# An order edge between each product of keys and receptances and the next, so that the halves of TensorE's rows take turns

## The chip, the cores and the metric

The kernel runs on one core of one Trainium2 chip. The metric is device time in microseconds (us). Times of the kernel before come from three runs; the profile is one more execution, and every duration below is from it.

## The reference

The model has seven stages over 256 tokens of width 2048, one batch, all float32: an RWKV-7 mixer (layer 0), a dilated attention (1), a pooling mixer (2), a second RWKV-7 mixer (3), a layer of attention and a linear recurrence (4), an mLSTM layer (5) and a final norm (6). The change lies in the two RWKV-7 mixers, in the part that computes this scan for 32 heads of 64:

```python
def _rwkv7_scan(r, w, k, v, a, b):
    """All inputs (B,S,H,N) float32. State S (B,H,N_v,N_k):
    S_t = S_{t-1} diag(w_t) + (S_{t-1} a_t) b_t^T + v_t k_t^T ;  y_t = S_t r_t."""
    ...
    def step(state, inp):
        r_t, w_t, k_t, v_t, a_t, b_t = inp
        sa = jnp.einsum('bhij,bhj->bhi', state, a_t)
        state = (state * w_t[:, :, None, :] + sa[..., None] * b_t[:, :, None, :]
                 + v_t[..., None] * k_t[:, :, None, :])
        y_t = jnp.einsum('bhij,bhj->bhi', state, r_t)
        return state, y_t
```

Around it stand four input projections (2048 x 2048 each, for r, k, v and the gate g), small low-rank products for decay and gates, a norm per head and an output projection (2048 x 2048).

## The kernel before

**Projections.** `proj` (L262) multiplies in three fp32r products (high by high, high by low, low by high). Each weight block of 512 KB is fetched by a DMA queued on SyncE (`wr`), split by ScalarE into its high part (`wh`, L220) and by VectorE, in the RWKV layers at times GpSimd, into its low part (`wl`, L221), and feeds 12 products of 128x128 by 128x512 on TensorE. These products are the filler of TensorE's queue through the whole program.

**The scan by blocks.** `rwkv_block` treats 4 heads (256 columns) at a time, so a layer has 8 blocks; `rwkv_blocks` starts one about every 40 us of the planner's time, and several are under way at once. The 256 tokens of a block are 4 chunks of 64. A block computes its decays and gates; builds `AR` (receptances and removal keys, scaled) and `BK` (keys and their counterparts, scaled), last of all by GpSimd (L811); computes the bonus product into the PSUM tile `qb` (L824), which ScalarE copies out as `bon` (L828); multiplies `BK` by `AR` within each chunk (L838, the lines of the change); masks the result into `GM` on VectorE (L841); copies the small diagonal blocks to `Md` (ScalarE, L856); inverts them by a recurrence on VectorE (L867 to L877), a product chain (L925, L952) on TensorE; and walks over the chunks (L986 to L1018). `yt` is then normed and joined into `z` (L1032 to L1053), transposed (L277) and used by `w_out`, the output projection. Block 7's part of `z` feeds only the last quarter of `w_out`.

**The products of L838.** The two heads of a pair lie on partitions 0 to 63 and 64 to 127. For each pair `f` (0, 1) there are 8 products, chunk c = 0..3 by half hp = 0, 1; each contracts over 64 rows, so it uses one half of TensorE's rows. The four of a half go to one PSUM tile (`qs[hp]`), and `qs` are of the pool `tp`, which has two banks. `tp` also holds `qb`, the transposes (L277, L785) and the low-rank products (L720). A float32 product is two passes on the chip, so the profile counts 512 passes for the 2 layers x 8 blocks x 2 pairs x 8 products = 256.

**What sets the order.** The program text is not the order of the queues. A scheduler (the tile framework, with a timeline model) places each instruction on its engine's queue when its inputs are ready by its model, by priority; blocks of the scan have a high priority (`urgent`). Queues then run in order on the chip.

Of the kernel before, what the change touches and what calls it, by code (L numbers as in the profile page):

```python
# [23 lines left out]
ORDER = mybir.DependencyInfo(mybir.DependencyClass.NoSync, mybir.DependencyReason.DATA)  # L24
# [90 lines left out]
class Builder:  # L115
# [558 lines left out]
    def rwkv_block(self, ia, b):  # L674

        nc, I, S = self.nc, self.I, self.S
# [89 lines left out]
        AR = self.t("q4", [128, 2, 4, 128], F32, 8)  # L766
        BK = self.t("q4", [128, 2, 4, 128], F32, 8)
# [54 lines left out]
        for t in range(2):  # L822
            for f in range(2):
                nc.tensor.matmul(qb[:, t * 4 + f * 2:t * 4 + f * 2 + 2], pr[:, f, t * 128:t * 128 + 128], rkc[:, f],  # L824
                                 start=True, stop=True)
# [6 lines left out]
        gmask = self.c("gmask")  # L832
        for f in range(2):
            qs = [self.p("tp", (128, 4, 128)) for _ in range(2)]
            for c in range(4):
                for hp in range(2):
                    rs = slice(hp * 64, hp * 64 + 64)
                    nc.tensor.matmul(qs[hp][:, c], BK[rs, f, c], AR[rs, f, c], start=True, stop=True)  # L838
            self.pe(0.9)
            for hp in range(2):  # L840
                nc.vector.tensor_tensor(GM[:, f * 2 + hp].rearrange("p (q a) n -> p q (a n)", a=2),  # L841
                                        qs[hp].rearrange("p (q a) n -> p q (a n)", a=2),
                                        gmask[:, f * 128:f * 128 + 256].unsqueeze(1).to_broadcast([128, 2, 256]), OP.mult)
            yield 1.0
# [7 lines left out]
        for i in range(4):  # L852
            rs = slice(i * 32, i * 32 + 32)
# [115 lines left out]
        rows = self.bcast(I["a_rows"][ia, b, 256:768], "rows", 512, 1)  # L969
# [3 lines left out]
        for c in range(4):  # L973
# [18 lines left out]
            for hp in range(2):  # L992
                for f in range(2):
                    nc.tensor.matmul(gy[ar[f], 4 + hp], X[ar[f], (f * 2 + hp) * 2 + pq], G[ar[f], f, hp],
                                     start=first, stop=True, skip_group_check=True)
# [5 lines left out]
            if c < 3:  # L1001
                for hh in range(4):
                    f, hp = hh // 2, hh % 2
                    nc.tensor.matmul(gy[half[hp], 6 + f], BT[:, f * 3 + c, half[hp]], UV[:, hh * 64:hh * 64 + 64],
                                     start=first, stop=True, skip_group_check=True)
# [10 lines left out]
            for hh in range(4):  # L1016
                f, hp = hh // 2, hh % 2
                nc.tensor.matmul(gy[kr[f], hh], GM[:, hh, c, to[f]:to[f] + 64], UV[:, hh * 64:hh * 64 + 64],  # L1018
                                 start=first, stop=True, skip_group_check=True)
# [838 lines left out]
```

## Time and profile before

| | us |
|---|---|
| median of three runs | 3241.56 |
| the three runs | 3240.18, 3241.56, 3243.27 |
| profiled execution, its own time | 3250.24 |
| its span, first to last instruction | 3247.1 |
| TensorE busy | 3034.3 (93%) |
| VectorE busy | 2304.0 (71%) |
| ScalarE busy | 1783.2 (55%) |
| mean granted TensorE clock | 0.967 |

The profiled execution took 8.7 us more than the median, and 3.1 us of it lie outside the span. Layer 0's scan runs from about 180 to 740 us of the span, layer 3's from about 1800 to 2400 us. Views of the profile name an instruction by its line, its engine, and the tiles that it writes and reads, buffer numbers left out. PE is TensorE, PEld its weight loads, DVE VectorE, ACT ScalarE, POOL GpSimd. An engine's busy time counts a product until its modelled end, so the step from one start to the next start is the better measure of what a run of products occupies.

### The profile page before, as it was taken

The page shows a single profiled execution, that of the slowest core. Times are in us where ns is not written, and L with a number is a line of the kernel's source. Part 1 is how long each engine was busy: PE and PEld are TensorE (multiplying, and loading weights), DVE is VectorE, ACT ScalarE, POOL GpSimd, SP SyncE. Part 2 cuts the span into 40 slices and gives each one's busy share as a digit, 9 for nine tenths or more (in the row PEclk, how much of TensorE's full clock was granted, in tenths as well). Part 3 has the DMA queues.
Part 4 walks back from the last instruction along what each step waited for, and adds up shares of the span by engine and source line. Part 5 has one row for each costly group of instructions (what it writes and reads, how often), then busy time and mean ns, then how long its engine had stood idle before and what let it go on. Part 6 is the DMA issues. An engine that isn't in the chain of part 4 may idle for free. (4 is left out here: it accounts for less than half of the span.)

```text
span 3247.1 us, 48857 instructions
## 1 busy us (share of the span) xinstructions
PE 3034.3 (93%) x17128; PEld 2452.2 (76%) x17128; DVE 2304.0 (71%) x4623; ACT 1783.2 (55%) x3504; POOL 794.6 (24%) x614
## 2 busy tenths in 40 slices
PE   6889999998999999999978898998989999999998
PEld 4667677776888888888856776777777788888886
DVE  7778778765666666676597788788557775666765
ACT  4565555444555555655555565554456765555554
POOL 4433443440112111020054325434312110000101
PEclk9999999999999999999989998999999999999999
DMA  5654453366666656666656644533665566666665
GB/s 186 200 193 145 155 175 121 122 200 203 178 174 178 177 169 205 205 211 191 208 174 219 197 152 153 171 119 105 206 214 160 156 188 203 182 199 172 186 187 169
DMA packets 327014, 577.24 MB, mean 178 GB/s; under 512 B 33856, under 2 KB 60776, under 8 KB 326768
## 3 DMA queue, kind: packets, MB, share of 16 engines
q1 hardware_dynamic: 326768, 574.12, 57.4%
q8 instruction: 134, 2.20, 0.3%
q14 instruction: 112, 0.92, 0.1%
HBM read 527.88 MB, written 46.15 MB: 177 GB/s over the span
## 5 line engine op out<-in xcount | busy, mean ns | idle before, releaser
L221 DVE TENSOR_TENSOR wl<-wr,wh 128x512 fp32r<-128x512 f32 x1580 | 1179.0, 758 | 690.8 <-ACT wh L220 664.3
L220 ACT CAST wh<-wr 128x512 fp32r<-128x512 f32 x1728 | 1052.4, 620 | 976.2 <-PE qps L262 452.9
L262 PE MATMUL qps<-wl,ah 128*128 128x512 f32 x3424 | 1385.8, 405 | 39.1 <-DVE wl L221 38.2
L262 PE MATMUL qps<-wh,al 128*128 128x512 f32 x3424 | 1368.7, 400 | 1.3 <-DVE al L221 1.3
L262 PE MATMUL qps<-wh,ah 128*128 128x512 f32 x3424 | 1266.3, 405 | 45.7 <-ACT wh L220 13.2
L262 PEld LDWEIGHTS qps<-wh,ah 128*128 128x128 f32 x3424 | 656.5, 192 | 191.0 <-ACT st L596 15.4
L262 PEld LDWEIGHTS qps<-wl,ah 128*128 128x128 f32 x3424 | 659.0, 192 | 187.2 <-DVE wl L221 53.3
L262 PEld LDWEIGHTS qps<-wh,al 128*128 128x128 f32 x3424 | 657.5, 192 | 137.9 <-DVE al L221 2.7
L221 POOL TENSOR_TENSOR wl<-wr,wh 128x512 fp32r<-128x512 f32 x148 | 203.6, 1385 | 363.9 <-ACT wh L220 336.3
L1103 POOL TENSOR_TENSOR q<-q,gain 128x1024 f32<-128x1024 f32 (+1 forms) x15 | 35.0, 2332 | 376.5 <-ACT sq L1097 376.5
L321 POOL TENSOR_TENSOR rstd<-rs_v,mhalf 128x2 f32<-128x2 f32 x7 | 5.0, 708 | 430.6 <-DVE rs_v L319 430.5
L277 PE MATMUL qtp<-cst,q 128*128 128x128 f32 x388 | 62.0, 289 | 23.0 <-DVE al L295 6.8
L838 PE MATMUL qtp<-q,q 64*128 64x128 f32 x512 | 72.4, 306 | 7.5 <-DVE GM L841 3.8
L277 PEld LDWEIGHTS qtp<-cst,q 128*128 128x128 f32 x388 | 48.5, 148 | 36.5 <-issue 20.5
L485 DVE SCALAR_TENSOR_TENSOR e<-q,vec,q 128x256 f32<-128x256 f32 x96 | 73.7, 811 | 0.0
L872 DVE TENSOR_TENSOR mb<-mb,Xc 128x120 f32<-128x120 f32 (+14 forms) x240 | 73.1, 305 | 0.1
L838 PEld LDWEIGHTS qtp<-q,q 64*128 64x128 f32 x512 | 57.9, 201 | 18.3 <-POOL q L811 5.1
L221 DVE TENSOR_TENSOR al<-st,ah 128x512 fp32r<-128x512 f32 x64 | 54.7, 871 | 23.5 <-ACT ah L220 23.4
L856 ACT COPY Md<-GM 32x128 f32<-32x128 f32 x128 | 55.3, 432 | 27.7 <-DVE GM L841 26.4
L220 ACT CAST ah<-st 128x512 fp32r<-128x512 f32 x64 | 38.3, 617 | 57.6 <-DMA st<-mix 49.7
L875 DVE TENSOR_TENSOR Xc<-Xc,mb 128x8 f32<-128x8 f32 x240 | 59.2, 247 | 1.1
L487 POOL TENSOR_TENSOR e<-e,q 128x512 f32<-128x512 f32 x32 | 48.2, 1521 | 31.8 <-ACT e L483 27.0
(388 smaller groups left out, 3383.2 us busy)
## 6 DMA issues: line engine op xcount, KB each, us to landing
wr<-a_w_in SPq DMA_DIRECT2D x256, 512.0 KB
wr<-b_w_in SPq DMA_DIRECT2D x160, 512.0 KB
wr<-odd_w_in SPq DMA_DIRECT2D x128, 512.0 KB
wr<-even_w_in SPq DMA_DIRECT2D x72, 512.0 KB
wr<-a_w_out SPq DMA_DIRECT2D x64, 512.0 KB
wr<-c_w_in SPq DMA_DIRECT2D x64, 512.0 KB
st<-mix SPq DMA_DIRECT2D x64, 256.0 KB
wr<-c_w_out SPq DMA_DIRECT2D x32, 512.0 KB
```

What stands on the lines that cost most here:

```text
L220: self.nc.scalar.copy(hi, src)
L221: (eng or self.nc.vector).tensor_tensor(lo, src, hi.bitcast(F32), OP.subtract)
L262: nc.tensor.matmul(o[:, cs], u[:, kk, sl], v[k][:, cs], start=st and x == 0 and c1 == 0, stop=sp and x == 2, skip_group_check=True)
L277: nc.tensor.transpose(q[:, f, t * 128:t * 128 + 128], src[:, t, (fp * 2 + f) * 128:(fp * 2 + f) * 128 + 128], self.ident)
L321: nc.gpsimd.tensor_tensor(r, v, self.mhalf[:, 0:2], OP.pow)
L485: ins = nc.vector.scalar_tensor_tensor(m[:, f], st.xx[c][:, ft], mu, st.h[c][:, ft], OP.mult, OP.add)
L487: ins = nc.gpsimd.tensor_tensor(m, m, st.h[c][:, a * 2:a * 2 + 2], OP.add)
L838: nc.tensor.matmul(qs[hp][:, c], BK[rs, f, c], AR[rs, f, c], start=True, stop=True)
L856: nc.scalar.copy(Md[rs, :, us].rearrange("p c u -> p u c"), GM2[rs, us, (1 - i // 2) ^ f, rs])
L872: nc.vector.tensor_tensor(mb[:, 0:n], mb[:, 0:n], Xc[:, r:r + 1].to_broadcast([128, n, 8]), OP.mult)
L875: nc.vector.tensor_tensor(Xc[:, r + 1], Xc[:, r + 1], mb[:, 0], OP.add)
L1103: nc.gpsimd.tensor_tensor(e3, e3, gain.unsqueeze(1).to_broadcast([128, 2 * nh, 128]), OP.mult)
```

## The change

Each product of L838 gets an order edge to the one before it within its pair `f`. The edge is between instructions of one engine, with no semaphore; it only tells the scheduler that the second may not be placed ahead of the first. As the loop goes over hp within c, the halves of the rows take turns: 0, 1, 0, 1, and so on. In the changed kernel the products are at L839, and all lines behind them stand 4 higher.

```diff
         for f in range(2):
             qs = [self.p("tp", (128, 4, 128)) for _ in range(2)]
+            turn = None
             for c in range(4):
                 for hp in range(2):
                     rs = slice(hp * 64, hp * 64 + 64)
-                    nc.tensor.matmul(qs[hp][:, c], BK[rs, f, c], AR[rs, f, c], start=True, stop=True)
+                    mm = nc.tensor.matmul(qs[hp][:, c], BK[rs, f, c], AR[rs, f, c], start=True, stop=True)
+                    if turn is not None:
+                        self.tc.add_manual_dep(mm.ins, turn.ins.name, ORDER, reason="the halves of the rows take turns")
+                    turn = mm
             self.pe(0.9)
```

No instruction is added or removed, on any engine. The scheduler's result moves between the first block and the end of the scan in each of the two layers, on all five queues; outside these two stretches the queues are the same but for a handful of rows. In TensorE's queue of 14,374 products, the 256 products of L838 stand in 71 unbroken runs before and in 64 now. Within the runs, 119 products followed one of the same half before, and none does now.

The first place is TensorE's queue at block 2 of layer 0, first pair: `qtp_3355` and `qtp_3356` are its two halves. Before, first the one half,

```order
L1004 MATMUL qgy_2362<-uv_2366,q4_2155 64x64 x4
L262 MATMUL qps_2058<-wh_2268,ah_1827 128x512
L262 MATMUL qps_2058<-wl_2269,ah_1827 128x512
L262 MATMUL qps_2058<-wh_2268,al_1828 128x512
L262 MATMUL qps_2057<-wh_2339,ah_1920 128x512
L838 MATMUL qtp_3355<-q4_3221,q4_3222 128x128 x4
```

and 22 products later the other, the four of a half together each time:

```order
L262 MATMUL qps_2058<-wl_2344,ah_1920 128x512
L262 MATMUL qps_2058<-wh_2343,al_1921 128x512
L262 MATMUL qps_2057<-wh_2398,ah_1920 128x512
L262 MATMUL qps_2057<-wl_2399,ah_1920 128x512
L262 MATMUL qps_2057<-wh_2398,al_1921 128x512
L262 MATMUL qps_2058<-wh_2398,ah_1920 128x512
L262 MATMUL qps_2058<-wl_2399,ah_1920 128x512
L838 MATMUL qtp_3356<-q4_3221,q4_3222 128x128 x4
L925 MATMUL qgm_2932<-Y_2930,GM_2689 64x64 x5
```

Now the first product stands at about the same place, alone, and the other seven follow 155 products later, behind work of the blocks before (L956 is the old L952, L998 the old L994):

```order
L998 MATMUL qgy_2501<-G_2507,X_2209 64x64 x4
L956 MATMUL qgm_3041<-X_2928,W_3005 32x32 x15
L839 MATMUL qtp_3356<-q4_3221,q4_3222 128x128
L839 MATMUL qtp_3355<-q4_3221,q4_3222 128x128
L839 MATMUL qtp_3356<-q4_3221,q4_3222 128x128
L839 MATMUL qtp_3355<-q4_3221,q4_3222 128x128
L839 MATMUL qtp_3356<-q4_3221,q4_3222 128x128
L839 MATMUL qtp_3355<-q4_3221,q4_3222 128x128
L839 MATMUL qtp_3356<-q4_3221,q4_3222 128x128
```

What moved is the completion of the first pair. Before, both halves went one after the other through one bank of `tp` while the other bank still held `qb`; now both banks are needed at once, and the second product waits for `bon`'s copy out of `qb`. In 12 of the 16 blocks 20 or more products stand between the first product of the first pair and its second (20 to 155).

The second place is ScalarE's queue at the copy `bon` of block 1 of layer 0. Before:

```order
L903 COPY AV_2161<-qgm_2162 128x512
L828 COPY bon_2687<-qtp_2682 128x8
L220 CAST ah_1827<-st_1829 128x512
L220 CAST ah_1827<-st_1833 128x512
L220 CAST wh_1906<-wr_1904 128x512
L911 COPY q4_2155<-qgm_2185 128x384
L220 CAST wh_1910<-wr_1904 128x512
L856 COPY Md_2738<-GM_2689 32x4x32 x4
```

Now (L907, L915 and L860 are the old L903, L911 and L856):

```order
L907 COPY AV_2161<-qgm_2162 128x512
L915 COPY q4_2155<-qgm_2180 128x384
L828 COPY bon_2687<-qtp_2682 128x8
L220 CAST ah_1827<-st_1833 128x512
L220 CAST wh_1906<-wr_1904 128x512
L220 CAST wh_1910<-wr_1904 128x512
L220 CAST wh_1961<-wr_1959 128x512
L915 COPY q4_2155<-qgm_2185 128x384
L220 CAST wh_1965<-wr_1959 128x512
L860 COPY Md_2738<-GM_2689 32x4x32 x4
```

The copies `Md` moved back against `bon`. Before, the first `Md` copy stood ahead of `bon` in 6 of the 16 blocks (2, 3, 6 and 7 of layer 0, 2 and 4 of layer 3); now `bon` is first in all of them.

The third place is the end of each scan in TensorE's queue, told in counts. Layer 0: between block 7's last chunk product (L1018) and the transposes of its `z` (L277) stood 72 products of L262, and now 98; the chunk product itself stands at the same place as before. Layer 3: there stood 91, and now 59; the chunk product stands 72 products later than before.

## Rows read from the trace of the kernel before

**Rows 1.** The page: the span, and busy time of each engine over it.

```profile
span 3247.1 us, 48857 instructions
PE 3034.3 (93%) x17128; PEld 2452.2 (76%) x17128; DVE 2304.0 (71%) x4623; ACT 1783.2 (55%) x3504; POOL 794.6 (24%) x614
```

**Rows 2.** Stretches of both scans: length, busy us by engine, PEclk granted clock, DMA.

```profile
core 0: us, PE busy (x) PEld busy (x) DVE busy (x) ACT busy (x) POOL busy (x), PEclk, DMA share, GB/s
...
180.00:740.00 560.00, 519.66 (x3989) 408.25 (x3988) 435.16 (x1201) 297.83 (x653) 228.09 (x184) 0.95 0.50 157
...
1800.00:2400.00 600.00, 549.02 (x4134) 432.18 (x4133) 455.55 (x1260) 316.27 (x690) 236.54 (x187) 0.94 0.52 165
```

**Rows 3.** ScalarE's waits, 1800 to 2400: who for whom, us, times, longest.

```profile
ACT wh L220 <- PE qps L262: 82.2, 67, 6.1
```

**Rows 4.** The page's groups of L838: busy, mean ns of one, idle before, releaser.

```profile
L838 PE MATMUL qtp<-q,q 64*128 64x128 f32 x512 | 72.4, 306 | 7.5 <-DVE GM L841 3.8 <-POOL q L811 3.7
...
L838 PEld LDWEIGHTS qtp<-q,q 64*128 64x128 f32 x512 | 57.9, 201 | 18.3 <-POOL q L811 5.1 <-issue 4.9 <-DVE GM L841 4.2
```

**Rows 5.** Timeline of PE, 183.7 to 185.8: start, us, instruction, count.

```profile
183.71 0.39 PE L262 MATMUL qps<-wh,al 128*128 128x512 f32 x1
183.94 0.39 PE L262 MATMUL qps<-wh,ah 128*128 128x512 f32 x1
184.25 1.16 PE L838 MATMUL qtp<-q,q 64*128 64x128 f32 x16
185.34 0.50 PE L262 MATMUL qps<-wl,ah 128*128 128x512 f32 x1
185.69 0.39 PE L262 MATMUL qps<-wh,al 128*128 128x512 f32 x1
```

**Rows 6.** Timeline of PE at two runs of a single half.

```profile
1962.04 0.49 PE L838 MATMUL qtp<-q,q 64*128 64x128 f32 x2 [0.16 <-POOL q L811]
1962.46 0.71 PE L986 MATMUL qgy<-S,q 128*128 128x128 f32 x4
...
2229.72 1.16 PE L838 MATMUL qtp<-q,q 64*128 64x128 f32 x8
2230.80 0.50 PE L262 MATMUL qps<-wh,ah 128*128 128x512 f32 x1
```

**Rows 7.** Timeline of block 2 in layer 0: bonus product, L838, mask, `bon`.

```profile
260.29 0.95 PE L824 MATMUL qtp<-rkc,e 128*128 128x2 f32 x8
...
269.11 1.16 PE L838 MATMUL qtp<-q,q 64*128 64x128 f32 x8 [0.88 <-POOL q L811]
277.10 0.68 DVE L841 TENSOR_TENSOR GM<-qtp,cst 128x512 f32<-128x512 f32 x1
...
277.83 1.16 PE L838 MATMUL qtp<-q,q 64*128 64x128 f32 x8 [2.15 <-DVE GM L841]
...
292.41 0.17 ACT L828 COPY bon<-qtp 128x8 f32<-128x8 f32 x1
```

**Rows 8.** Stretches behind two such waits, columns as in Rows 2.

```profile
225.00:233.00 8.00, 6.17 (x39) 4.80 (x41) 7.37 (x11) 5.71 (x14) 6.19 (x6) 0.57 0.55 172
277.00:284.00 7.00, 5.84 (x55) 4.70 (x56) 5.50 (x11) 3.47 (x8) 0.00 (x0) 0.76 0.36 117
```

**Rows 9.** Timeline at the ends of both scans: last chunk product, `z`, its transposes.

```profile
713.44 0.46 PE L1018 MATMUL qgy<-uv,GM 128*64 128x64 f32 x8
...
733.39 0.65 PE L277 MATMUL qtp<-cst,z 128*128 128x128 f32 x4 [2.43 <-DVE z L1051]
734.68 0.77 PE L262 MATMUL qps<-wh,ah 128*128 128x512 f32 x1 [0.64 <-ACT ah L220]
...
2339.52 0.46 PE L1018 MATMUL qgy<-uv,GM 128*64 128x64 f32 x8
...
2361.03 0.68 DVE L1051 SCALAR_TENSOR_TENSOR z<-yt,z 128x512 f32<-128x512 f32 x1
2363.88 0.60 PE L277 MATMUL qtp<-cst,z 128*128 128x128 f32 x4
```

## The prediction

> **What bounds the kernel now.** I read the page first, then the stretches, then the waits. The page gives TensorE 93% of the span [rows 1], so time taken from it is the first candidate for time gained. The change touches only two stretches, the scans of layers 0 and 3. There TensorE is busy 519.7 of 560 us and 549.0 of 600 us, 92 to 93%, and VectorE 435.2 and 455.6 us, 76 to 78% [rows 2]. The weight splits tell which of the two leads: in layer 3's stretch ScalarE waited 82.2 us for TensorE to let go of weight buffers [rows 3], its largest wait there. The feed is ahead of TensorE more often than behind it. So a microsecond less of TensorE's work is mostly a microsecond less of time, but not wholly: the 7 to 8% in which TensorE stood idle are waits on VectorE, ScalarE and DMAs, which stay as long as they are.
>
> L838 itself is busy 72.4 us over both layers, with 7.5 us of idle time before it [rows 4].
>
> **What taking turns saves.** Eight products (16 passes) whose halves alternate occupy TensorE from 184.25 to 185.34, 1.09 us [rows 5]. Four products (8 passes) of one half occupy it from 2229.72 to 2230.80, 1.08 us, and one product alone from 1962.04 to 1962.46, 0.42 us [rows 6]. So a further product of the same half costs (1.08 - 0.42) / 3 = 0.22 us, a run has 0.20 us of its own, and two products of different halves next to each other cost what one costs: eight in turns are four steps, 0.20 + 4 x 0.22 = 1.08, as measured. Around a run the neighbours lose a little: L262 products start 0.23 apart, but 0.31 passes before the run and 0.35 after it [rows 5], so 0.08 + 0.12 = 0.20 us more. A run costs 0.40 us plus 0.22 for each step.
>
> Counting the runs of the two orders with each alternating pair as one step, I find 217 steps in 71 runs before and 149 steps in 64 runs now. That is 68 x 0.22 = 15.0 us, and 7 x 0.40 = 2.8 us, together 17.8 us less of TensorE's work. It isn't the 256 to 128 steps that the idea suggests: four of the 32 groups alternated fully before, others in part, and now the first product of a group often stands alone, which makes a run and a step of its own.
>
> [...]
>
> How much of the 17.8 us becomes time? The ends are nothing (another engine or a chain's latency takes each microsecond) and all of it. With TensorE busy for 92% of both stretches and the weight splits waiting for it [rows 2, 3], I take three quarters: **13.4 us less**.
>
> **What the new order costs inside the scans.** Before, the two halves of a group could use one bank of `tp` after the other: in block 2 the second half waited 2.15 us for the mask of the first [rows 7]. This wait, 3.8 us in all [rows 4], goes, since both halves finish together. In its place the second product waits for the copy `bon`. In block 2 of the kernel before, that copy came at 292.41, 32 us after its product at 260.29, and it delayed nothing then [rows 7]; now the whole group hangs on it. TensorE's queue runs in order, so if `bon` is late, the products of all blocks under way and L262 stand behind it, and then VectorE's masks and the `Md` copies. The scheduler has put the second product far back for this (12 blocks with 20 to 155 products in between), so by its model the wait is over. [...] Below nothing, the old mask waits bring 3.8. [...] I take **2 us more**: one or two late copies, less the mask waits. The value is near the low end, since ScalarE is busy about half of these stretches (297.8 of 560 us, 316.3 of 600 [rows 2]) and `bon` is a copy of 0.17 us [rows 7].
>
> **The ends of the scans.** From the last chunk product to the finished `z` it took 19.9 us in layer 0 (713.44 to the wait's end near 733.3) and 22.2 us in layer 3 (2339.52 to 2361.03 + 0.68) [rows 9]. This chain is on VectorE, ScalarE and GpSimd and does not get shorter. TensorE covers it with L262. In layer 0 the cover was 72 products, which ended 2.43 us too early, and a wait of 0.64 us came behind [rows 9]. Now it is 98 products, at least 98 x 0.23 = 22.5 us, so the 3 us of waiting go: **3 us less**, and the slower clock behind them is left as a reserve. In layer 3 the cover was 91 products in 24.4 us, 0.27 each, and hid the chain. Now it is 59: 13.6 us at 0.23 each, 15.9 at 0.27. TensorE then waits between 19.9 - 15.9 = 4.0 and 22.2 - 13.6 = 8.6 us, with up to 1.7 us of slow clock behind it as after the other waits [rows 8]. I take **6 us more**, near the middle.
>
> **Edits at nothing.** The edges add no semaphore and no instruction. The rows of the DMA queue that changed places fetch the same weights; the shared cover for them is the three buffers of `wr`. Should this fail, it shows as ScalarE waiting for `wr`.
>
> **The sum.** -13.4 + 2 - 3 + 6 = -8.4 us. Against the profiled execution's own 3250.2 us (the span is 3247.1) this gives 3241.8; the median lay 8.7 us below that execution, so on its side I expect 3241.6 - 8.4 = 3233.2, say 3233 us. About 0.2%, 6.5 us, is what a measurement of this kernel can tell from no change, so the forecast lies just beyond it.
>
> **Rivals.**
>
> *The gain is taken by the feed (no change).* VectorE is at 76 to 78% in the scans and has the recurrence and all the low parts of the weights in one queue [rows 2]. If TensorE's saved time only lengthens its waits on them, the conversion is a quarter: -4.5 + 2 - 3 + 6 = +0.5 us, 3242 us. For it: the rescheduled queues differ everywhere in the scans, and 7 to 8% of idle time shows that a block's latency already counts. Against it: the 82 us that the splits waited for TensorE [rows 3].
>
> [...]
>
> *The edges don't do what they say.* The order of the changed kernel excludes it: all 32 groups read 0, 1, 0, 1.
>
> *The gain is whole.* With all 17.8 us, no late copy and the mask waits gone: -17.8 - 3.8 - 3 + 4 = -20.6, 3221 us. It is the low end of the forecast rather than a case of its own.
>
> **How the numbers follow.** Forecast, a gain of 7 to 21 us: 0.46. No change: 0.28. Slower by the late copies or a longer uncovered end in layer 3: 0.26. The range reaches from the whole gain, with 3 us for what the clock gives back, 3218, to a little below the slower rival's time, 3256, so that about one in ten lies on either side. The forecast's own range is 3218 to 3235, and the other two cases hold more than half of the chance together. Chances: faster by over 0.2% 0.46, within 0.2% 0.28, slower by over 0.2% 0.26.
>
> **What would show it.** In the profile after, L839's busy time should fall from 72.4 us to about 50 to 56, and whole groups of 16 passes should take 1.1 us. TensorE's wait for the mask (`GM`) should be gone. [...] Before the `z` transposes of layer 3's block 7 a wait of 4 to 9 us should stand, and in layer 0 none. TensorE's other idle time in the two stretches should not grow by more than about 4 us; if it grows by 13, the feed has taken the gain. The prediction would be wrong from the ground if L839's time didn't fall, or if the two stretches took the same time with less work in them.

## The result and the profile after

The changed kernel took **3277.41 us** (median of four runs, 3273.34 to 3279.61) against 3242.41 for the kernel before in the same batch: ratio 1.0105, 95% interval 1.0088 to 1.0122. It is 35 us slower, where 8 us faster was forecast. Repeated in a later batch it took 3272.26, ratio 1.0084 [1.0057, 1.0111].

The page after, span and busy time, to hold against [rows 1]:

```profile
span 3274.1 us, 48894 instructions
PE 3021.2 (92%) x17128; PEld 2434.5 (74%) x17128; DVE 2320.2 (71%) x4623; ACT 1784.4 (55%) x3504; POOL 797.1 (24%) x614
```

TensorE works 13.1 us less and the span is 27.0 us longer, so its idle time grew by 40.1 us (212.8 to 252.9). (The two profiled executions differ by 27 us and the medians by 35, since the one of the kernel before lay 8 us above its median.) VectorE works 16.2 us more, with the same instructions. The page's groups say where (line, engine, tiles, shapes, count, busy us, mean ns, idle before and releaser). After:

```profile
L876 DVE TENSOR_TENSOR mb<-mb,Xc 128x120 f32<-128x120 f32 (+14 forms) x240 | 80.4, 335 | 0.2
L879 DVE TENSOR_TENSOR Xc<-Xc,mb 128x8 f32<-128x8 f32 x240 | 77.4, 323 | 0.9
...
L839 PE MATMUL qtp<-q,q 64*128 64x128 f32 x512 | 52.7, 299 | 5.4 <-POOL q L811 3.2
```

and the same two VectorE groups in the kernel before:

```profile
L872 DVE TENSOR_TENSOR mb<-mb,Xc 128x120 f32<-128x120 f32 (+14 forms) x240 | 73.1, 305 | 0.1
L875 DVE TENSOR_TENSOR Xc<-Xc,mb 128x8 f32<-128x8 f32 x240 | 59.2, 247 | 1.1
```

The products fell from 72.4 [rows 4] to 52.7 us, as the change meant them to. The recurrence on VectorE rose from 132.3 to 157.8 us, 25.5 more, though it does the same.

Most of the loss lies in layer 3. The operation `sq` of ScalarE starts for the first time in layer 1, behind layer 0's scan, and for the last time in layer 4, behind layer 3's. Its line gives both starts, before and then after:

```profile
L1097 ACT ACTIVATE sq<-q x15: 656/1067/1098, 816.7 to 2567.7; 128x1024 f32<-128x1024 f32 x14, 128x512 f32<-128x512 f32 x1
```

```profile
L1101 ACT ACTIVATE sq<-q x15: 656/1067/1097, 822.9 to 2594.7; 128x1024 f32<-128x1024 f32 x14, 128x512 f32<-128x512 f32 x1
```

The program is 6 us late behind the first scan and 27 us behind the second.

The view of TensorE's waits says what the new idle time waits for (who for whom: us, times, longest). Kernel before, 180 to 745:

```profile
PE qgm L925 <- DVE Y L934: 2.6, 2, 1.5
PE qtp L277 <- DVE z L1051: 2.4, 1, 2.4
PE qgy L994 <- DVE G L989: 2.3, 3, 1.2
```

After, the same stretch (L998, L929 and L990 are the old L994, L925 and L986):

```profile
PE qgy L998 <- DVE X L959: 11.3, 2, 6.8
PE qgm L929 <- DVE Y L938: 10.3, 4, 8.8
PE qgy L998 <- DVE G L993: 6.7, 3, 3.9
...
PE qps L262 <- DVE st L387: 5.2, 1, 5.2
PE qgy L990 <- DVE S L1019: 5.1, 2, 3.5
```

All five are waits for VectorE, four of them in the inverse and the chunk walk of a block. The wait for `X` did not exist before. Other rows fell: before, the chunk walk's wait for `uv` (L1004) was the largest with 7.2 us, and now it is 0.8; all rows of the stretch together grew from 39.7 to 61.4 us. In layer 3 (1800 to 2440) they grew from 54.6 to 70.1, and the largest row there, before and then after, is a wait for a DMA, of weights for the low-rank products:

```profile
PE qtp L720 <- DMA lw<-a_a2x: 12.8, 7, 3.4
```

```profile
PE qtp L720 <- DMA lw<-a_a2x: 20.0, 7, 6.0
...
PE qtp L839 <- ACT bon L828: 2.1, 1, 2.1
```

The second row is the wait for `bon`, which the forecast feared: TensorE stood for it once in the whole program, 2.1 us. Yet `bon` is where the delay begins. Timeline of block 2 of layer 0, first pair, to hold against [rows 7]:

```profile
272.83 0.49 PE L839 MATMUL qtp<-q,q 64*128 64x128 f32 x2
...
291.98 1.04 POOL L1033 TENSOR_TENSOR vt<-vt,bon 128x512 f32<-128x512 f32 x1 [6.39 <-ACT uv L984]
...
293.06 0.17 ACT L828 COPY bon<-qtp 128x8 f32<-128x8 f32 x1 [0.44 <-POOL vt L1033]
...
298.31 1.16 PE L839 MATMUL qtp<-q,q 64*128 64x128 f32 x14
...
299.30 1.29 DVE L845 TENSOR_TENSOR GM<-qtp,cst 128x512 f32<-128x512 f32 x2
```

`bon` has two buffers, so the copy of block 2 needs the buffer that block 0 still uses: it starts 0.04 us after GpSimd's last use of it (L1033, `vt` times `bon`, at the end of block 0's chunk walk). The pair is complete at 299.5; before, it was complete at 279.0. TensorE is not idle meanwhile, since the scheduler put other work there; the block is late instead. In 7 of the 12 blocks that have a block two ahead, `bon` now starts within 0.4 us after that block's last use; before, in 3.

Before, in blocks 2, 3, 6 and 7 of layer 0, both pairs were done when `bon` came, since the halves passed through the bank that `qb` did not hold. In block 2 the second pair ended at 289.2, and `bon` came at 292.41 [rows 7]:

```profile
288.68 0.49 PE L838 MATMUL qtp<-q,q 64*128 64x128 f32 x2
```

The recurrence began only 2.1 to 5.3 us after `bon` in these four blocks. Now first pair, masks, `Md` copies and second pair all stand behind the copy, and it begins 17.1 to 24.9 us after `bon` in all 16 blocks. So the blocks follow each other more slowly: from the recurrence of block 0 to that of block 7 it took 408.2 us in layer 0 and 407.8 in layer 3, and now 418.7 and 438.2.

That moves a block's recurrence to the time when GpSimd norms the output of the block two ahead (`yt`, L1038 to L1049). A piece of block 3's recurrence beside block 1's `yt`, timeline of VectorE and GpSimd after:

```profile
384.84 1.28 POOL L1047 TENSOR_TENSOR yt<-yt,rows 128x512 f32<-128x512 f32 x1
...
385.00 1.15 DVE L879 TENSOR_TENSOR Xc<-Xc,mb 128x8 f32<-128x8 f32 x1
...
386.20 0.20 DVE L876 TENSOR_TENSOR mb<-mb,Xc 128x56 f32<-128x56 f32 x1
386.20 1.35 POOL L1048 TENSOR_TENSOR yt<-yt,rows 128x512 f32<-128x512 f32 x1
...
386.44 1.13 DVE L879 TENSOR_TENSOR Xc<-Xc,mb 128x8 f32<-128x8 f32 x1
...
387.62 0.20 DVE L876 TENSOR_TENSOR mb<-mb,Xc 128x48 f32<-128x48 f32 x1
...
387.85 0.17 DVE L879 TENSOR_TENSOR Xc<-Xc,mb 128x8 f32<-128x8 f32 x1
```

The `Xc` operation by itself took 0.17 us here, and the two beside a GpSimd operation took 1.13 and 1.15; each ended just behind that one (386.15 behind 386.12, 387.57 behind 387.55). Of the 480 operations of these two groups 73 took over 0.6 us, 47 before, and every one of them overlaps a GpSimd operation. Of these, 26 lie longest beside `yt`, 7 before; the others lie mostly beside the low parts `wl` (40, and 34 before).

### The profile page after: what moved, and what is told of

It reads as the page before. It is cut to its first block, busy times and chain, and to the rows that moved or that the text cites. A ratio compares the mean times of both kernels' runs of the same rounds, so it can differ in the third digit from the quotient of the medians.

```text
span 3274.1 us, 48894 instructions
## 1 busy us (share of the span) xinstructions
PE 3021.2 (92%) x17128; PEld 2434.5 (74%) x17128; DVE 2320.2 (71%) x4623; ACT 1784.4 (55%) x3504; POOL 797.1 (24%) x614
## 5 line engine op out<-in xcount | busy, mean ns | idle before, releaser
L262 PE MATMUL qps<-wl,ah 128*128 128x512 f32 x3424 | 1388.3, 406 | 40.9 <-DVE wl L221 39.9
L262 PE MATMUL qps<-wh,al 128*128 128x512 f32 x3424 | 1369.4, 401 | 1.3 <-DVE al L221 1.3
L262 PE MATMUL qps<-wh,ah 128*128 128x512 f32 x3424 | 1264.6, 405 | 45.8 <-DVE st L387 12.2
L262 PEld LDWEIGHTS qps<-wl,ah 128*128 128x128 f32 x3424 | 659.4, 193 | 191.8 <-DVE wl L221 57.6
L262 PEld LDWEIGHTS qps<-wh,ah 128*128 128x128 f32 x3424 | 656.5, 192 | 192.5 <-issue 24.2
L262 PEld LDWEIGHTS qps<-wh,al 128*128 128x128 f32 x3424 | 659.2, 193 | 138.3 <-DVE al L221 3.3
L277 PE MATMUL qtp<-cst,q 128*128 128x128 f32 x388 | 62.0, 289 | 23.1 <-DMA cst<-consts 6.9
L876 DVE TENSOR_TENSOR mb<-mb,Xc 128x120 f32<-128x120 f32 (+14 forms) x240 | 80.4, 335 | 0.2
L879 DVE TENSOR_TENSOR Xc<-Xc,mb 128x8 f32<-128x8 f32 x240 | 77.4, 323 | 0.9
L277 PEld LDWEIGHTS qtp<-cst,q 128*128 128x128 f32 x388 | 48.6, 148 | 36.5 <-issue 19.7
L860 ACT COPY Md<-GM 32x128 f32<-32x128 f32 x128 | 54.9, 429 | 17.8 <-DVE GM L845 16.6
L577 POOL TENSOR_TENSOR GM<-e,GM 128x512 fp32r<-128x512 f32 x32 | 53.7, 1697 | 17.8 <-ACT GM L576 17.8
L839 PE MATMUL qtp<-q,q 64*128 64x128 f32 x512 | 52.7, 299 | 5.4 <-POOL q L811 3.2
```

The costliest lines, as they stand in the source:

```text
L262: nc.tensor.matmul(o[:, cs], u[:, kk, sl], v[k][:, cs], start=st and x == 0 and c1 == 0, stop=sp and x == 2, skip_group_check=True)
L277: nc.tensor.transpose(q[:, f, t * 128:t * 128 + 128], src[:, t, (fp * 2 + f) * 128:(fp * 2 + f) * 128 + 128], self.ident)
L577: nc.gpsimd.tensor_tensor(hl[:, 1, s], m, hl[:, 0, s].bitcast(F32), OP.subtract)
L839: mm = nc.tensor.matmul(qs[hp][:, c], BK[rs, f, c], AR[rs, f, c], start=True, stop=True)
L860: nc.scalar.copy(Md[rs, :, us].rearrange("p c u -> p u c"), GM2[rs, us, (1 - i // 2) ^ f, rs])
L876: nc.vector.tensor_tensor(mb[:, 0:n], mb[:, 0:n], Xc[:, r:r + 1].to_broadcast([128, n, 8]), OP.mult)
```

## Experiments

Each table lists the median, the ratio to the kernel before in the same batch with its interval, the busy time of the products (the group of L838 or L839), the recurrence's VectorE time (sum of the two groups above), and the slow recurrence operations beside GpSimd's `yt`; times are in us. Where nothing else is said the edit is to the changed kernel (with turns) or, "no turn", to the kernel before.

### Four buffers of `bon`, with and without the turns

```diff
-        bon = self.t("bon", [128, 8], F32, 2)
+        bon = self.t("bon", [128, 8], F32, 4)
```

> The changed kernel with four buffers in place of two for the small tile bon. In both profiles bon's copy of block b starts 0.1 us after the GpSimd product that last reads bon of block b-2 (L1029) in most blocks, so two buffers tie it to the end of block b-2. Theory (the turns hang the first pair on bon's copy, and bon on block b-2; the delayed masks and recurrences make TensorE wait): the tie is gone, the first pair is complete 1 to 10 us after its first product, and the 35 us of loss come back, with the shorter products on top: 3225 to 3245 us. Rival (the loss is only that some thousand instructions stand in another order, whatever ties them): no reason for a return, 3260 to 3290 us.

> The kernel before with four buffers for bon and no turns: the control. Theory: the halves could use one bank after the other, so bon's delay cost little before: 3232 to 3245 us. Rival (rearranged queues as such): it rearranges thousands of instructions as well and may land 20 us or more off, 3220 to 3275 us.

| | median | ratio | products | recurrence | beside `yt` |
|---|---|---|---|---|---|
| kernel before | 3242 | 1 | 72.4 | 132.3 | 7 |
| changed | 3277.4 | 1.0105 [1.0088, 1.0122] | 52.7 | 157.8 | 26 |
| e1, turns, four | 3257.1 | 1.0056 [1.0041, 1.0071] | 52.3 | 135.5 | 9 |
| e2, no turn, four | 3241.0 | 1.0005 [0.9992, 1.0017] | 58.9 | 132.1 | 8 |

Untied, the turns lose about half as much, which lies between what the two theories expected of e1. (The expectation says that `bon` follows the last use two blocks earlier in most blocks of both kernels; counted, it is 7 of 12 after and 3 before.) The timeline of e1 in block 2 shows the copy ahead of the pair, and the pair in one piece:

```profile
268.63 0.18 ACT L828 COPY bon<-qtp 128x8 f32<-128x8 f32 x1
...
272.82 1.16 PE L839 MATMUL qtp<-q,q 64*128 64x128 f32 x16
```

The recurrence is back at its old time. But 18 us of loss stay, with 20 us less of products than before. In e2, whose queues are drawn anew as well, 13.5 us less of products brought no time.

### One pair only

The edges only for `f == 1` (e3) or only for `f == 0` (e4).

```diff
-                    if turn is not None:
+                    if turn is not None and f == 1:
```

> The changed kernel with the edges on the second pair (f = 1) alone, whose banks come free by the masks of the first pair and not by bon. Theory: no loss, and about a third to a half of the saved TensorE work: 3232 to 3246 us. Rival (rearranged queues): loss of half the size or more, 3255 to 3280 us.

> The changed kernel with the edges on the first pair (f = 0) alone, which hangs on bon. Theory: nearly the whole loss stays, 3265 to 3285 us, with the first pair complete only after bon. Rival (rearranged queues): between the two kernels, 3245 to 3270 us.

e3 took 3253.3, 1.004 [1.0024, 1.0056], products 62.2, recurrence 139.8, 13 beside `yt`; e4 3266.7, 1.0087 [1.0071, 1.0102], 49.7, 150.8 and 24. The first pair carries the tie and most of the loss. e3 should have lost nothing by the theory; it lost 13 us, nearly what the rival expected.

### The bonus product in another pool

`qb` leaves `tp`, so that no product of a pair waits for `bon`'s copy.

```diff
-        qb = self.p("tp", (128, 512))
+        qb = self.p("gm", (128, 512))
```

> The changed kernel with the bonus product in a bank of the pool gm in place of tp, so that bon's copy no longer holds a bank that the turns need; to be read against e6, the same without turns. Theory of the tie (bon's bank alone makes the turns dear): e5 within 6 us of e6 or below it. Theory of the spread (any other order of the queues moves the time by 10 to 20 us either way, and that is what is left of the loss in e1 and e3): e5 and e6 are 10 us or more from before, each with its own sign.

> The kernel before with the bonus product in gm: the control of e5. Theory of the tie: 3230 to 3250 us. Theory of the spread: anywhere from 3225 to 3270 us.

With turns (e5) 3249.7, 1.0031 [1.0018, 1.0043], products 51.5; without (e6) 3253.6, 1.0029 [1.0015, 1.0044], products 50.7, since with both banks free the scheduler alternates by itself. There is no longer a difference between turns and none. `gm` is a pool of the chain itself, and its lost bank, or the new order alone, may be what costs the 10 us in both; that was not tried.

### The queues held, only the products changed

Here all five queues are written out as order edges from instruction to instruction, so that nothing else moves. e9: queues of the kernel before, each product issued twice. e10: queues of e6, products within each run sorted by half. e12: queues of the changed kernel, products within each run sorted by half. In these three kernels the lines stand one or more further down.

```diff
+                    m1 = nc.tensor.matmul(qs[hp][:, c], BK[rs, f, c], AR[rs, f, c], start=True, stop=True)
+                    m2 = nc.tensor.matmul(qs[hp][:, c], BK[rs, f, c], AR[rs, f, c], start=True, stop=True)
...
+        keep_queues(nc, tc, b.more)
```

> The five queues of the kernel before, held instruction by instruction with order edges, and each product of L838 issued twice in its place: 256 more products in the same half, 256 x 0.22 = 56 us more of TensorE's work, nothing else moved. If TensorE's time in the scans is time (the step of the prediction that took three quarters): 35 to 60 us slower, 3275 to 3300 us. If the scans are bound by the chain of the blocks and TensorE's idle time takes such a change: less than 15 us slower, 3238 to 3255 us.

> The five queues of e6, held, with the products inside each unbroken run of L838 sorted by half, so that no two neighbours alternate: 216 steps in place of 152, 64 x 0.22 = 14 us more of TensorE's work, and no instruction outside these runs moved. If TensorE's time is time: 9 to 15 us above e6 (ratio to before 1.0057 to 1.0076). If not: within 4 us of e6.

> The five queues of the changed kernel, held, with the products inside each unbroken run sorted by half: 217 steps in place of 149, 15 us more of TensorE's work, nothing outside the runs moved. It takes the taking of turns away and leaves the new order. If TensorE's time is time: 9 to 16 us above the changed kernel, 3283 to 3295 us; then the order alone costs some 45 us and the turns give 12 back. If not: within 4 us of the changed kernel, and the turns themselves are worth nothing here.

e9 took 3266.8, 1.0066 [1.0040, 1.0092]. The products' busy time rose by 50.4 us (122.8 for 72.4; 56 were expected) and the kernel lost 21 by the ratio, so 0.4 of such work becomes time. Its page says where much of the rest went: TensorE's idle time fell by 17.7 us (195.1 for 212.8). The recurrence, 133.0 us with 7 beside `yt`, stayed as it was. e10 took 3252.0, 1.0034 [1.0018, 1.0050], no different from e6, with products of 61.0 us for 50.7. e12 took 3279.4, 1.0111 [1.0089, 1.0133], beside 1.0084 [1.0057, 1.0111] for the changed kernel in that batch; the intervals leave open whether its longer products cost anything. Its groups:

```profile
L839 PE MATMUL qtp<-q,q 64*128 64x128 f32 x512 | 63.2, 297 | 4.7 <-POOL q L812 3.0 <-ACT bon L829 1.8
```

The sorting undid only half of the saving: 10.5 of 19.7 us in e12, and 10.3 in e10, where 15 and 14 were expected. The timeline of e12 at its first group, four products of one half and then four of the other, says why:

```profile
183.16 1.71 PE L839 MATMUL qtp<-q,q 64*128 64x128 f32 x16
184.80 0.50 PE L263 MATMUL qps<-wl,ah 128*128 128x512 f32 x1
```

The group occupies TensorE for 1.64 us. By the prediction's steps, eight products one after the other would take 0.20 + 8 x 0.22 = 1.96, and a group in turns took 1.09 [rows 5]. That is 0.32 us less than one after the other, so by this estimate the halves overlapped where they met, though the queue has them one behind the other.

e12 decides the main point all the same. It has no turns inside a run and gives half of the saving away, yet it is as slow as the changed kernel (recurrence 155.4, 25 beside `yt`). What lost the time is the new order of the queues, not how the products run.

### Other orders: PERIOD 42 and 38

`PERIOD` is the planner's time between the starts of two blocks. A change of it by 5% draws another order, with nothing else altered.

```diff
-PERIOD = 40.0
+PERIOD = 42.0
```

> The kernel before with blocks started every 42 us of the planner's time in place of 40: other queues, nothing else changed, the control of e8. Theory of the tie: near before, 3230 to 3250 us. Theory of the spread: 10 us or more away from before.

> The changed kernel with the same 42 us, which keeps bon in tp with two buffers. Theory of the tie: 20 to 40 us above e7, as after is above before. Theory of the spread: less than 12 us from e7, or below it.

> The changed kernel with the planner's PERIOD 42 in place of 40 and four buffers of bon in place of two. Against the same with two buffers (e8, 3265 us). Theory, the tie of a block's first pair to the chunk walk two blocks earlier costs in every order: 10 to 20 us lower than e8, so 3245 to 3255. Rival, the tie cost only in the one order that the changed kernel happened on: within 8 us of e8 on either side, 3257 to 3273.

> The kernel before with PERIOD 38, no turns, 216 steps of the products on TensorE (217 before). Theory, the order that the planner gives is worth 10 to 30 us by itself and that of the kernel before is a favourable one: 3250 to 3270. Rival, only the turns cost: 3235 to 3245.

> The changed kernel with PERIOD 38, 148 steps, bon with two buffers. Theory, the turns save some 15 us of TensorE work of which under half arrives, and the tie takes 10 to 20 back: 0 to 15 us above e14. Rival, the tie is luck: e14 less 0 to 8 us.

> As e15 with four buffers of bon, 146 steps. Theory, tie: 10 to 20 us lower than e15. Rival, luck of the order: within 8 us of e15, on either side.

| | median | ratio | recurrence | beside `yt` |
|---|---|---|---|---|
| e7, 42, no turn | 3266.7 | 1.0083 [1.0057, 1.0109] | 135.7 | 13 |
| e8, 42, turns | 3265.1 | 1.0069 [1.0046, 1.0092] | 148.8 | 18 |
| e13, 42, turns, four | 3243.6 | 1.0016 [1.0001, 1.0030] | 136.7 | 9 |
| e14, 38, no turn | 3244.7 | 1.0006 [0.9990, 1.0023] | 130.0 | 8 |
| e15, 38, turns | 3272.5 | 1.0105 [1.0085, 1.0125] | 149.1 | 22 |
| e16, 38, turns, four | 3266.3 | 1.0081 [1.0059, 1.0104] | 135.7 | 6 |

Four buffers give back 0.0049 of the time at 40, 0.0053 at 42 and 0.0024 at 38: 16, 17 and 8 us, the last with intervals that overlap. Against the repeat of the changed kernel (1.0084) the return at 40 is 9 us, and the intervals just overlap too. Four buffers without turns, the control that e2 is at 40, were not run at 42 and 38. The recurrence falls each time, by 12 to 22 us.

But an order by itself also moves the time: e7 loses 27 us with no tie added, e14 nothing, and e16 loses 26 with the tie gone. Several expectations failed on this: e8 should have been 20 to 40 us above e7 and is no slower, e14 was expected slower than it is, e15 lost more than either theory had, and e16 stayed within the 8 us of e15 that the rival named.

I find no single row that explains e7 and e16, but the pages tell them apart. In e7 TensorE was busy 14.0 us longer than in the kernel before (3048.3 us) with the same products, and idle only 4.7 longer; its mean granted clock was 0.963 for 0.967, and 0.004 of its span of 3265.8 us is 13 us, an estimate of what the clock makes of the 14. The clock was 0.963 in e16 and in e13 too. In e16 TensorE was busy 2.2 us less, with products of 53.9 us for 72.4, and idle 20.4 us longer (233.2). Its blocks are not late: from the recurrence of block 0 to that of block 7 it takes 390.0 and 391.1 us, less than before. The wait for the DMA `lw` in layer 3 is 17.6 and 17.5 us in the two, 12.8 before; but it is 17.2 in e13 too, which hardly loses, and what delays these loads was not tried.

### One buffer of `bon`

The tie made one block shorter: with turns a pair then hangs on the end of the block just ahead. Without turns `qb` holds one bank, the pairs pass through the other, and only the next block's `qb` is held up.

```diff
-        bon = self.t("bon", [128, 8], F32, 2)
+        bon = self.t("bon", [128, 8], F32, 1)
```

> The changed kernel with one buffer of bon in place of two, so that a block's first pair can be finished only when the block ahead has ended its walk over the chunks, and not the one two ahead. Theory, the tie is a cost of the turns: from a block's bon to its last yt it takes some 130 us by the trace of the changed kernel, against 40 us from block to block, so a layer's eight blocks come nearly one after the other: several hundred us slower, 3600 to 4500. Rival, the number of buffers only draws another order: 3240 to 3300.

> The kernel before with one buffer of bon. Without turns a pair needs only one bank of tp, so a late bon holds one bank and the products pass through the other; only the next block's qb fills that too, which ties a block to the end of the one two ahead, as the turns do with two buffers. Theory, tie: 10 to 40 us slower than the kernel before, 3250 to 3280, far below e17. Rival, one buffer of bon is what costs, with turns or without: as slow as e17.

e17 (turns) took 3450.2, 1.0636 [1.0578, 1.0695]; e18 (no turn) 3285.9, 1.0130 [1.0069, 1.0191], two runs each. The several hundred us expected of e17 were too many, the order of the two was right. Timelines of block 1 of layer 0, e17:

```profile
227.00 0.65 PE L839 MATMUL qtp<-q,q 64*128 64x128 f32 x2 [0.38 <-POOL q L811]
...
287.63 1.05 POOL L1033 TENSOR_TENSOR vt<-vt,bon 128x512 f32<-128x512 f32 x1
...
288.77 0.17 ACT L828 COPY bon<-qtp 128x8 f32<-128x8 f32 x1
...
291.06 1.16 PE L839 MATMUL qtp<-q,q 64*128 64x128 f32 x14
```

and e18:

```profile
228.63 2.07 PE L838 MATMUL qtp<-q,q 64*128 64x128 f32 x8 [2.01 <-POOL q L811]
...
235.66 1.16 PE L838 MATMUL qtp<-q,q 64*128 64x128 f32 x8
...
292.35 1.04 POOL L1029 TENSOR_TENSOR vt<-vt,bon 128x512 f32<-128x512 f32 x1
...
293.42 0.17 ACT L828 COPY bon<-qtp 128x8 f32<-128x8 f32 x1 [2.84 <-POOL vt L1029]
```

Both copies of `bon` come where block 0's walk ends. With turns the pair waits 64 us for it; without, the pair is done at 236.8, long before. e18 also shows the tie of the changed kernel made without turns: block 2's bonus product (290.6 us) and first pair (296.8) stand at the end of block 0, its recurrence operations beside `yt` rise to 28, and the recurrence takes 157.6 us, as in the changed kernel (157.8). It loses 42 us. In e17 the recurrence takes only 126.5 us (18 beside `yt`), less than in the kernel before, while the kernel loses 206 us: a late start of the blocks costs without any slower recurrence.

## Why the prediction was wrong

**The saving of the products was right.** 17.8 us were worked out from steps and runs; the group fell by 19.7 us of busy time, to 52.7, inside the 50 to 56 named as the sign.

**How much of it becomes time was wrong.** Three quarters were taken from TensorE's 92% and the splits that waited for it [rows 2, 3]. With the queues held, 0.4 of such work became time in e9 and none that can be measured in e10. The rival "the feed takes the gain" had that step nearer: e9's added products took 17.7 us out of TensorE's idle time, so shorter ones may well lengthen it, though no run shows that by itself. The sign named for this rival came too: TensorE's idle time in the two stretches, which should not have grown by more than about 4 us, grew by 37 (21.7 and 15.5), for whatever reason.

**The price of `bon` was looked for in the wrong place.** This is the step that failed. I saw that the second product waits for `bon`, and priced it as TensorE standing there. No run shows the 2 us more that the sum takes for this: TensorE stood once, for 2.1 us, and with the mask waits of 3.8 us gone that is 1.7 us less. I read the 20 to 155 products that the scheduler put in between as the cure. They were the cost: a block's first pair, and all behind it, now comes after the end of the block two ahead. [Rows 7] held the sign of it: `bon` 32 us after its product. I took that for a late ScalarE; the reason was the buffer, whose user two blocks earlier I didn't look up. The chance given to "slower by the late copies" had the right copy and the wrong mechanism, waits of TensorE for `bon`. The upper end of the range, 3256 us, rests on a price of such waits that no run shows either. The loss was larger, and the part of it that `bon` explains came by blocks that start late.

**The clash with GpSimd was not in the prediction at all.** The recurrence takes 25.5 us more. Of its operations 26 are slow beside the older block's `yt`, 7 before; by an estimate, their time in the two traces less 0.19 us each (the mean of the operations up to 0.6 us), these make 18 of the 25.5 us, and those beside `wl` 6. That the tie brings the slow operations beside `yt` is shown in three orders and by e18. That it costs time is shown at 40 and 42 (16 and 17 us) and not resolved at 38 (8 us). How much of this price is the slower recurrence and how much the late start is not shown: e17 has the late start alone.

**The mask waits went**, as forecast: no wait of TensorE for `GM` at these products is left among its waits at L839. The gain of 3.8 us was real and small.

**The ends of the scans.** The forecast was -3 us in layer 0 and +6 in layer 3. The timeline of TensorE after, layer 0's end and then layer 3's:

```profile
717.81 0.46 PE L1022 MATMUL qgy<-uv,GM 128*64 128x64 f32 x8
...
739.99 0.77 PE L262 MATMUL qps<-wh,ah 128*128 128x512 f32 x1 [5.18 <-DVE st L387]
...
747.71 0.60 PE L277 MATMUL qtp<-cst,z 128*128 128x128 f32 x4
```

```profile
2386.76 0.46 PE L1022 MATMUL qgy<-uv,GM 128*64 128x64 f32 x8
...
2397.37 0.73 PE L262 MATMUL qps<-wh,ah 128*128 128x512 f32 x2 [2.00 <-ACT wh L220]
...
2404.93 0.47 PE L262 MATMUL qps<-wh,ah 128*128 128x512 f32 x1 [3.02 <-DVE st L387]
...
2409.32 0.61 PE L277 MATMUL qtp<-cst,z 128*128 128x128 f32 x4
```

In layer 0 the wait for `z` [rows 9] went, but the cover of 98 products itself stopped 5.18 us for VectorE's `st`: from the last chunk product (717.8) to the transposes it took 29.9 us for 98 x 0.23 = 22.5 us of products, 7.4 lost, where before about 20 us held 72 (16.6). So it was 4 us worse, not 3 better. In layer 3, 22.6 us hold 59 products (13.6), 9.0 lost, 5.6 more than before (24.4 us for 91 products, 20.9), near the 6 taken; but the waits stand on the feed, not at the `z` transposes where I had put them.

**The sum by its own steps.** Products about -8 (0.4 of 19.7) instead of -13; `bon` and the masks -2, and the tie +8 to +17, instead of +2 for both; the ends +10 instead of +3. That gives +8 to +17 of the 35 us, if the terms do not overlap. The rest, some 18 to 27 us, has the size of what e7 and e16 lose by nothing but another order, and there it stays: the kernel before has an order at the favourable end of those tried (3241 to 3267 us without turns), and any edit that draws a new one risks that much. What in those orders costs the time is open.

None of the kernels was faster than the kernel before. The best with turns, e13, stands at 1.0016.

## What to carry to other kernels

An order edge between instructions of one engine also ties the resources that each of them needs. When one makes two tiles needed at once, follow each tile to the buffer that must come free and its last user in an older piece of work; the price is then a late start of a whole chain, which no row of waits at that instruction shows. And where a scheduler draws the order anew after any edit, hold the queues fixed, or draw some more orders, before a gain or loss below 1% is put down to the edit.

## What the runs showed of the hardware

In these traces some of VectorE's small operations ended only behind a GpSimd operation. An `Xc` operation took 0.17 us alone and 1.13 to 1.15 beside one of `yt`. All 73 recurrence operations over 0.6 us in the changed kernel overlap GpSimd and end 0.02 to 0.14 us behind the end of one of its operations, and the longest took 1.35 us; in the kernel before the same holds of all 47 over 0.6 us. Not every operation that overlapped was slow: 94 short ones (23% of the rest) overlap as well, and 74 of these had begun first or lie beside GpSimd's `rg_y`, `rk_y` and `z`.

On TensorE, products of different halves next to each other started 4 to 14 ns apart in the kernel before and 5 to 8 in the changed one, and a pair of passes took 0.11 us from its start to the next pair's, as long as one pass of the same half: where the halves took turns, the rate was double. The saving of 19.7 us was 2% of the scans' work (519.7 and 549.0 us [rows 2]). By the estimate from the steps, two halves overlapped in part even when the queue had four products of one before four of the other (1.64 us for the eight in e12, 1.09 in turns).
